# RWKV's 64-row products on all four quarters of the array, and retention scores of two heads in turn

## The chip, the cores and the metric

The kernel runs on one core of one Trainium2 chip. The metric is device microseconds of one execution. Before the change the median of three runs is 1125.02 us (1124.61 to 1125.1).

## What is computed

Two decoder layers on a sequence of 256 tokens with 1024 channels, in fp32. Each layer has a mixing part, a cross-attention into 256 memory tokens, and an MLP of 4096. The mixing part projects the normalised input once and hands the columns to four branches of 256 channels each (4 heads of 64): sparse attention, retention, RWKV-7, and a short convolution. Each branch is projected to 1024 channels, gated, summed, and projected once more.

The change touches two branches. RWKV-7, per head, token by token:

```python
def step(state, inp):
    r_t, w_t, k_t, v_t, kk_t, a_t = inp
    sa = jnp.einsum('bhvk,bhk->bhv', state, -kk_t)
    state = (state * w_t[:, :, None, :]
             + sa[..., None] * (kk_t * a_t)[:, :, None, :]
             + v_t[..., None] * k_t[:, :, None, :])
    return state, jnp.einsum('bhvk,bhk->bhv', state, r_t)
```

Retention, per head and chunk of 128 tokens:

```python
att = jnp.einsum('bhld,bhmd->bhlm', qc, kc) * inner_decay
o = (jnp.einsum('bhlm,bhmd->bhld', att, vc)
     + jnp.einsum('bhld,bhde->bhle', qc, state) * q_decay[None, :, :, None])
```

## The kernel before, in words

**The large matmuls.** Nearly all weights are streamed as units of 512 KB and split on the chip into a high part (ScalarE) and a low part (VectorE), both in the fp32r format; each product is three matmuls (`mm3`: high x high, high x low, low x high). They are the bulk of TensorE's work. In the profile they write tiles named `A`, `C` or `S`.

**The order.** Nothing runs in the order in which it is written. Every operation goes into a list (`Sched.add`) with a cost on its engine, and `Sched.run` plans the order: at each step it takes the operation that can start first by its model, and among those the one with the lowest rank. The projections have rank 9; RWKV is put in at rank 1 (its side products at 1.5), sparse attention at 2, retention at 3. So a product of RWKV goes as soon as its inputs are there, and the projections fill the time between. `together` makes one operation of several matmuls, which then follow each other on TensorE, and gives it one cost. The tiles `B` (two banks of PSUM at a time) are RWKV's, `C` those of sparse attention and retention.

**RWKV (`rwkv`).** The recurrence is done in chunks of 64 tokens: 256 tokens are two halves `t`, each of two chunks, and a tile of 128 partitions holds the even chunk on partitions 0 to 63 and the odd chunk on 64 to 127 (`par2`). The index `m = 4 t + h` (0 to 7) is the half and the head. All of it is plain fp32. Per layer and in the order of the work:

- scores `low` and `AL` (lines 1139 to 1149): for each head parity `s`, which is a half of the partitions of `ra` and `bb`, one group of 8 products of 64 x 64 x 64; each product writes to the chunk's half of the bank's partitions;
- `amat` (lines 1151 to 1163): the same with 128 columns, once for `AB` and, at rank 1.5 in `side`, once for `AK`, each as two groups of 8;
- the inverses of the 8-row blocks `R` and `RT` on VectorE and TensorE, which don't change;
- `mulc` (lines 1213 to 1221): 16 products of 64 x 64 x 64, the even chunk on rows 0 to 63 with its result on partitions 0 to 63 of one bank, the odd chunk on rows 64 to 127 with its result on partitions 64 to 127 of another bank. It makes the left half of the right side `rhs`, then `T1`, `RB` and `QB`;
- `RB` and `QB` are written as block-diagonal 128 x 128 matrices, zeros beside the blocks (four `memset` each, on GpSimd);
- `mul8` (lines 1205 to 1211): for each `m` one product of 128 x 128 x 128 with such a matrix, in two halves of four, each with its own bank and its own result. It makes `X1` and then, three times, `X = QB X + X1`; the sums are on VectorE;
- the states are carried from chunk to chunk (lines 1288 to 1317). After each odd chunk the output of both chunks of the half is made in one group: 16 products of 64 x 64 x 64, then the products of `ra` with the states, 128 rows by 64 by 128 columns (lines 1318 to 1332). The first chunk of all has no state.

**Retention (`ret`, lines 1536 to 1576).** For each head one bank of `C` takes the scores: a product of 64 x 128 x 256 and one of 64 x 128 x 128. Heads 0 and 2 lie on partitions 0 to 63, heads 1 and 3 on 64 to 127. The four heads are separate operations, so the planner orders them.

`self.act` is ScalarE's copy (line 621 in the profile), `self.tt` VectorE's two-operand operation (line 632), `self.vcopy` VectorE's copy (line 655), `self.mm` a matmul (line 675), `self.tr` a transpose on TensorE (line 680).

Of the kernel before, what the change touches and what calls it, by code (L numbers as in the profile page):

```python
# [14 lines left out]
OP = mybir.AluOpType  # L15
# [5 lines left out]
T = 256  # L21
# [234 lines left out]
class V:  # L256
# [32 lines left out]
    def step(self, name, d, *a, **k):  # L289
        return V(self.t, self.steps + ((name, a, k),), d, self.box, self.dtype).bound()  # L290
# [306 lines left out]
class Prog:  # L597
# [89 lines left out]
            self.group.append((cost, out, ins, emit, cols))  # L687

    @contextmanager
    def together(self):  # L690
        if self.group is not None:
            yield
            return
        self.group = g = []
        yield
        self.group = None
        if g:
            cost = i = 0
            while i < len(g):
                a, b = g[i][1], g[min(i + 1, len(g) - 1)][1]  # L700
                if a.shape[0] == b.shape[0] == 64 and a.box[0] != b.box[0]:
# [349 lines left out]
    def rwkv(self, l, zr, zk, zv, zl):  # L1051
# [85 lines left out]
        par2 = (slice(0, 64), slice(64, 128))  # L1137

        low, up = self.tile([128, 8, 64], "g2"), self.tile([128, 8, 64], "g2")
        for s, po in enumerate(par2):  # L1140
            p = B((128, 4, 64))
            with self.together():
                for t in range(2):
                    for a in range(2):
                        for pr in par2:
                            self.mm(p[pr, 2 * t + a], ra[po, a, t, 1, pr],
                                    bb[po, a, t * 128 + pr.start:t * 128 + pr.stop])
            self.tt(low[:, s::2], p, bcn("own8l", 4), OP.mult)
            self.tt(AL[:, s::2], p, bcn("low16", 4), OP.mult)

        def amat(dst, src, mask, first):
            for s, po in enumerate(par2):
                p = B((128, 4, 128))
                with self.together():
                    for t in range(2):
                        for a in range(2):
                            for pr in par2:
                                self.mm(p[pr, 2 * t + a].rearrange("p (i u) -> p i u", i=2),
                                        src[po, a, t * 128 + pr.start:t * 128 + pr.stop], ra[po, a, t, :, pr])
# [42 lines left out]
        for a in range(2):  # L1202
            self.ts(indr[:, 2 * a:2 * a + 2], c["head2"], pcol(l, "rk", 1, a), pool=True)

        def mul8(lhsT, rhs, evac):
            for q in range(2):
                p = B((128, 4, 128))
                for i in range(4):
                    m = 4 * q + i
                    self.mm(p[:, i], lhsT[:, m], rhs[:, m])  # L1210
                evac(slice(4 * q, 4 * q + 4), p)

        def mulc(lhsT, rhs, evac):

            ps = [B((128, 8, 64)) for _ in range(2)]
            with self.together():
                for m in range(8):
                    for pr, p in zip(par2, ps):
                        self.mm(p[pr, m], lhsT[pr, m], rhs(pr, m))
            for pr, p in zip(par2, ps):  # L1220
                evac(pr, p[pr])


        vt = g2()
# [10 lines left out]
        def side():  # L1235

            tokmajor(lambda a, t: ra[:, a, t, 1, :],
                     lambda p: [self.act(rhs[:, 4 * t:4 * t + 4, 64:128], p[:, t].rearrange("p (h k) -> p h k", h=4))
                                for t in range(2)])
            def stack(m, rows):  # L1240
                return lambda p: [self.act(m[rows, i::2], p[pr]) for i, pr in enumerate(par2)]

            tokmajor(lambda a, t: bb[:, a, t * 128:t * 128 + 128], stack(KB, par2[1]))
            tokmajor(lambda a, t: zv[:, a, t * 128:t * 128 + 128],
                     lambda p: (self.act(vt, p), stack(VU, par2[0])(p)))
            amat(AK, kt, "mask_k", False)
            tokmajor(lambda a, t: kt[:, a, t * 128:t * 128 + 128], stack(KB, par2[0]))
            mulc(AK[:, :, 1, :], lambda pr, m: vt[pr, m // 4, 64 * (m % 4):64 * (m % 4) + 64],
                 lambda pr, p: self.act(rhs[pr, :, 0:64], p))
            p = B((128, 2, 4))  # L1250
            for t in range(2):
                for a in range(2):
                    self.mm(p[:, t, 2 * a:2 * a + 2], rk[:, a, t * 128:t * 128 + 128], indr[:, 2 * a:2 * a + 2])
            bon = self.small(8)
            self.vcopy(bon, p.rearrange("p t h -> p (t h)"))
            self.bon = bon

        self.at(1.5, side)
        T1 = self.tile([128, 8, 64], "g2")
        mulc(AB[:, :, 1, :], lambda pr, m: R[pr, m],  # L1260
             lambda pr, p: self.vcopy(T1[pr], p) if pr.start else self.act(T1[pr], p))
        RB, QB = (self.tile([128, 8, 128], "g4") for _ in range(2))
        for m in (RB, QB):
            for i in range(2):
                self.s.lead(self.memset(m[64 * i:64 * i + 64, :, 64 - 64 * i:128 - 64 * i], 0.0))
        mulc(T1, lambda pr, m: RT[pr, m], lambda pr, p: self.tt(RB[pr, :, pr], p, RT[pr], OP.add))
        mulc(AL, lambda pr, m: RB[pr, m, pr],
             lambda pr, p: self.vcopy(QB[pr, :, pr], p) if pr.start else self.act(QB[pr, :, pr], p))
        X1 = self.tile([128, 8, 128], "g4")
        mul8(RB, rhs, lambda s, p: self.act(X1[:, s], p))  # L1270
        X = self.tile([128, 8, 128], "g4")
        for i in range(3):
            mul8(QB, X if i else X1, lambda s, p: self.tt(X[:, s], p, X1[:, s], OP.add))
        self.dump("X", X)
        MTt = g2()
        mcs = []
# [13 lines left out]
        for ci in range(4):  # L1290
# [25 lines left out]
                for a in range(2):  # L1316
                    self.stt(Sn[:, a], src[:, a], P1[:, a, ci, 64:65], c["bd"], OP.mult, OP.mult)
            if par == 1:
                ys = [(pr, St, B((128, T))[pr]) for pr, St in zip(par2, (Sprev, S))]
                with self.together():  # L1320
                    for h in range(4):
                        hs, m = slice(64 * h, 64 * h + 64), 4 * t + h
                        for pr, St, y in ys:
                            self.mm(y[:, hs], AK[pr, m, 0, :], vt[pr, t, hs], h == 0, False)
                        for pr, St, y in ys:
                            self.mm(y[:, hs], AB[pr, m, 0, :], U[pr, t, hs], False, St is None and h == 3)
                    for a in range(2):
                        for pr, St, y in ys:
                            if St is not None:
                                self.mm(y[:, a * 128:a * 128 + 128], ra[:, a, t, 0, pr], St[:, a], False, a == 1)  # L1330
                for pr, _, y in ys:
                    self.act(o[pr, t], y)
            Sprev = S
            if ci < 3:
                S = Sn
# [200 lines left out]
    def ret(self, l):  # L1536
# [17 lines left out]
        o = COFF["dec"][0]  # L1554
        self.dma(dec.rearrange("p h m -> p (h m)"), self.cst[:, o:o + H * T])
        o = self.tile([128, 2, T], "g2")
        for h in range(4):
            a, po = h // 2, slice(64 * (h % 2), 64 * (h % 2) + 64)
            hs = slice(64 * h, 64 * h + 64)
            p = self.bank("C")  # L1560
            self.mm(p[:, 0:256], k[po, a, 0:128], q[po, a])
            self.mm(p[:, 256:384], k[po, a, 128:256], q[po, a, 128:256])
            at = self.tile([128, 384], "g2")
            self.tt(at[:, 0:256], p[:, 0:256], dec[:, h], OP.mult)
            self.tt(at[:, 256:384], p[:, 256:384], dec[:, h, 0:128], OP.mult)
            y = self.bank("C", (128, 2, 64))
            self.mm(y[:, 0], at[:, 0:128], tk1[:, 0, hs], True, True)
            self.mm(y[:, 1], at[:, 128:256], tk1[:, 0, hs], True, False)
            self.mm(y[:, 1], at[:, 256:384], tk1[:, 1, hs], False, True)
            self.act(o[:, :, hs], y)  # L1570
# [547 lines left out]
```

## Time and profile before

| | before |
|---|---|
| median of three runs | 1125.02 us |
| the profiled execution | 1125.16 us |
| its span, first to last instruction | 1123.4 us |
| TensorE busy (matmul records) | 1107.5 us, 99% |
| VectorE busy | 857.0 us, 76% |
| ScalarE busy | 653.2 us, 58% |
| GpSimd busy | 98.8 us, 9% |
| granted TensorE clock, mean | 0.998 |

In a row of the profile `B<-g,g 64*64 64x128 f32 x32` reads: written tile `B`, read tiles `g` and `g`, weights of 64 rows by 64 columns, moving data of 64 partitions by 128 columns, 32 records. A matmul of fp32 leaves two records, one of fp32r a single one. In the timeline, records in a row that write and read tiles of the same names are merged into one line with the form of the first; a line gives the start and the time until the last of them has ended. Records overlap, so the distance from the start of a line to the start of the next is the time that it takes in the stream. Times are in us from the start of the span.

### The profile page before, as it was taken

What the parts mean: (1) busy time and instruction counts of PE and PEld (TensorE: products, weight loads), DVE (VectorE), ACT (ScalarE), POOL (GpSimd) and SP (SyncE); (2) the same over time, 40 slices, a digit from 0 to 9 for tenths busy, and PEclk for the clock granted to TensorE, in tenths of its full rate; (3) what the DMA queues carried; (4) which work ended last, traced back from release to release, by engine and by line L of the source; (5) the groups of instructions that cost most, each with busy time, mean ns of one, the idle gap of its engine ahead of it and who ended that gap; (6) DMA issues with size and microseconds to landing.
All of it is one profiled execution on the core that took longest, in us unless ns stands there. A gap on an engine that the chain in (4) does not pass through costs nothing.

```text
span 1123.4 us, 19170 instructions
## 1 busy us (share of the span) xinstructions
PE 1107.5 (99%) x7354; PEld 976.4 (87%) x7354; DVE 857.0 (76%) x1318; ACT 653.2 (58%) x1049; POOL 98.8 (9%) x163
## 2 busy tenths in 40 slices
PE   9999999999999999999999999999999999999996
PEld 7899978788998899999889999988888987999995
DVE  5878785675858689888796689755757667998987
ACT  7555544545645567767664566444547455776673
POOL 3001010100200110000021001000002002000000
PEclk9999999999999999999999999999999999999999
DMA  8327546754537599998955154565655467899981
GB/s 328 118 72 242 172 152 191 257 189 150 187 131 244 185 278 270 264 275 244 295 168 156 35 182 155 183 189 187 226 185 170 144 217 216 249 267 281 260 255 51
DMA packets 75967, 225.26 MB, mean 201 GB/s; under 512 B 12223, under 2 KB 14015, under 8 KB 75748
## 3 DMA queue, kind: packets, MB, share of 16 engines
q1 hardware_dynamic: 71556, 208.31, 55.1%
q0 software_dynamic: 4320, 15.73, 8.5%
q8 instruction: 58, 0.95, 0.3%
q14 instruction: 33, 0.27, 0.1%
HBM read 221.90 MB, written 3.15 MB: 200 GB/s over the span
## 4 chain that ended last, share of the span: by engine, by line
PE 72%; DVE 3%; DMA 2%; ACT 2%; POOL 1%; issue 1%; POOLq 0%; DVEq 0%; SPq 0%; ACTq 0%
PE A L675 34%; PE C L675 17%; PE S L675 12%; PE B L675 8%; DMA g<-wts 2%; PE C L680 2%; DVE g L632 1%; ACT junk L621 1%; ACT g L621 1%; POOL s L644 1%; DVE x L638 0%; POOL s L666 0%; ACT hi L621 0%; DVE lo L632 0%; PE B L680 0%
## 5 line engine op out<-in xcount | busy, mean ns | idle before, releaser
L632 DVE TENSOR_TENSOR lo<-raw,hi 128x1024 fp32r<-128x1024 f32 (+1 forms) x308 | 368.7, 1213 | 99.3 <-ACT hi L621 73.4
L621 ACT ACTIVATE hi<-raw 128x1024 fp32r<-128x1024 f32 (+1 forms) x308 | 316.4, 1049 | 121.0 <-PE A L675 70.4
L675 PE MATMUL A<-hi,g 128*128 128x512 f32 (+2 forms) x1152 | 366.9, 389 | 0.8 <-ACT g L621 0.5
L675 PEld LDWEIGHTS A<-hi,g 128*128 128x128 f32 x1152 | 215.2, 188 | 46.9 <-issue 1.5
L675 PE MATMUL A<-lo,g 128*128 128x512 f32 (+2 forms) x576 | 221.2, 384 | 0.0
L632 DVE TENSOR_TENSOR g<-g,g 128x512 f32<-128x512 f32 (+3 forms) x218 | 188.2, 887 | 10.1 <-ACT g L621 8.8
L675 PE MATMUL A<-g,hi 128*128 128x256 f32 x928 | 177.6, 291 | 0.0
L621 ACT ACTIVATE g<-g 128x1024 fp32r<-128x1024 f32 (+7 forms) x224 | 147.6, 698 | 49.5 <-DVE g L632 23.8
L675 PE MATMUL C<-g,hi 128*128 128x256 f32 x960 | 173.1, 282 | 0.5 <-ACT g L621 0.5
L675 PEld LDWEIGHTS C<-g,hi 128*128 128x128 f32 x960 | 149.7, 188 | 3.2 <-ACT g L621 0.9
L675 PEld LDWEIGHTS A<-g,hi 128*128 128x128 f32 x928 | 143.9, 189 | 6.1 <-issue 4.3
L675 PE MATMUL C<-g,lo 128*128 128x256 f32 x480 | 135.7, 283 | 0.0
L621 ACT ACTIVATE g<-C 128x512 fp32r<-128x512 f32 (+4 forms) x119 | 59.4, 515 | 127.3 <-PE C L675 100.8
L675 PE MATMUL A<-g,lo 128*128 128x256 f32 x464 | 130.7, 282 | 0.4 <-DVE lo L632 0.4
L675 PEld LDWEIGHTS A<-lo,g 128*128 128x128 f32 x576 | 108.5, 188 | 20.7 <-issue 0.5
L675 PE MATMUL S<-g,g 128*128 128x512 f32 x450 | 109.8, 394 | 0.1
L675 PEld LDWEIGHTS S<-g,g 128*128 128x128 f32 x450 | 84.4, 188 | 20.3 <-DVE g L632 0.5
L675 PEld LDWEIGHTS C<-g,lo 128*128 128x128 f32 x480 | 90.4, 188 | 0.0
L675 PEld LDWEIGHTS A<-g,lo 128*128 128x128 f32 x464 | 87.7, 189 | 0.6 <-DVE lo L632 0.6
L621 ACT ACTIVATE g<-A 128x512 f32<-128x512 f32 (+3 forms) x70 | 39.8, 569 | 60.7 <-PE A L675 59.3
L675 PE MATMUL B<-g,g 64*64 64x64 f32 (+4 forms) x896 | 67.6, 253 | 0.8 <-DVE g L632 0.8
L675 PEld LDWEIGHTS B<-g,g 64*64 64x64 f32 (+2 forms) x896 | 58.8, 151 | 6.4 <-issue 1.4
(143 smaller groups left out, 1076.1 us busy)
## 6 DMA issues: line engine op xcount, KB each, us to landing
raw<-wts SPq DMA_DIRECT2D x300, 512.0 KB, 4.5
g<-wts SPq DMA_DIRECT2D x90, 256.0 KB, 5.4
g<-wts POOLq DMA_DIRECT2D x30, 512.0 KB, 5.8
g<-rows SPq DMA_DIRECT2D x11, 512.0 KB, 4.4
g<-memT SPq DMA_DIRECT2D x12, 256.0 KB, 6.0
g<-cmpw SPq DMA_DIRECT2D x4, 512.0 KB, 4.8
raw<-wts SPq DMA_DIRECT2D x4, 498.0 KB, 4.0
raw<-wts SPq DMA_DIRECT2D x4, 480.0 KB, 4.8
```

The costliest lines, as they stand in the source:

```text
L621: e = lambda: self.nc.scalar.activation(real(out), real(in_), func, bias=real(bias), scale=real(scale), accum_out=real(accum))
L632: f = lambda: e.tensor_tensor(real(out), real(a), real(b), op)
L644: f = lambda: e.tensor_scalar(real(out), real(a), real(s1), real(s2), op0=op0, **kw)
L675: e = lambda: self.nc.tensor.matmul(real(out), real(lhsT), real(rhs), start=start, stop=stop, skip_group_check=True)
L680: self.pe(0.109, out, [in_, self.ident], lambda: self.nc.tensor.transpose(real(out), real(in_), real(self.ident)), 128)
```

## The change

- `tiles` takes the place of the two loops over the head parity: the groups of both parities become one group, and within it the head parities (rows of the array) and the chunks (columns) change in turn, so that four products in a row lie on four different quarters of the array. Each parity keeps its own bank. `amat` uses it too.
- `quad` takes the place of `mulc` and `mul8`. Each of the 16 products (8 values of `m`, two chunks) is 64 x 64 x n. Even heads stay where they are: rows and result on the same half of the partitions, bank `pe`. Odd heads go to the other half: rows 0 to 63 to partitions 64 to 127 and the reverse, bank `po`. So an odd head's result lies on the other half of the partitions than its chunk.
- What follows copes with that: some results are kept on both halves (`T1s`, `QBs`, `X1s`, `Xs`, `RTs`), `mixed` takes the one that is needed, and `turn` copies a result back with two ScalarE copies of 64 partitions each. `RB` and `QB` are 64 x 64 blocks now, without zeros.
- The output group writes the even heads to one bank and the odd heads, turned, to another; the products with the states are cut into two of 64 columns.
- `together(True)` gives such groups a cost of a quarter of their columns.
- In `ret` the scores of two heads (partitions 0 to 63 and 64 to 127) become one group, in turn.

```diff
     @contextmanager
-    def together(self):
+    def together(self, quads=False):
...
+                if quads:
+                    cost += 4 * self.free(a) / 2400 + 0.01
+                    i += 3
-        for s, po in enumerate(par2):
-            p = B((128, 4, 64))
-            with self.together():
+        def tiles(src, n, dst):
+            with self.together(True):
                 for t in range(2):
                     for a in range(2):
-                        for pr in par2:
-                            self.mm(p[pr, 2 * t + a], ra[po, a, t, 1, pr],
-                                    bb[po, a, t * 128 + pr.start:t * 128 + pr.stop])
+                        for s, po in enumerate(par2):
+                            for pr in par2:
+                                self.mm(dst[s][pr, 2 * t + a], *src(t, a, po, pr))
...
-        def mul8(lhsT, rhs, evac):
-            for q in range(2):
-                p = B((128, 4, 128))
+        def quad(lhsT, rhs, n, swap=False):
+            pe, po = (B((128, 4, n)) for _ in range(2))
+            with self.together(True):
                 for i in range(4):
-                    m = 4 * q + i
-                    self.mm(p[:, i], lhsT[:, m], rhs[:, m])
-                evac(slice(4 * q, 4 * q + 4), p)
-        def mulc(lhsT, rhs, evac):
-            ps = [B((128, 8, 64)) for _ in range(2)]
-            with self.together():
-                for m in range(8):
-                    for pr, p in zip(par2, ps):
-                        self.mm(p[pr, m], lhsT[pr, m], rhs(pr, m))
-            for pr, p in zip(par2, ps):
-                evac(pr, p[pr])
+                    for pr in par2:
+                        self.mm(pe[pr, i], lhsT(pr, 2 * i), rhs(pr, 2 * i))
+                    for src, dst in zip(par2, par2[::-1]):
+                        self.mm(po[dst, i], lhsT(src, 2 * i + 1), rhs(src, 2 * i + 1))
+            return pe, po
+        at = lambda m: lambda pr, i: m[pr, i]
+        mixed = lambda m, odd: lambda pr, i: odd[pr, i // 2] if i % 2 else m[pr, i]
+        def turn(dst, src):
+            for d, s in zip(par2, par2[::-1]):
+                self.act(dst[d], src[s])
...
-            mulc(AK[:, :, 1, :], lambda pr, m: vt[pr, m // 4, 64 * (m % 4):64 * (m % 4) + 64],
-                 lambda pr, p: self.act(rhs[pr, :, 0:64], p))
+            pe, po = quad(at(AK[:, :, 1, :]), lambda pr, m: vt[pr, m // 4, 64 * (m % 4):64 * (m % 4) + 64], 64)
+            self.act(rhs[:, 0::2, 0:64], pe)
+            turn(rhs[:, 1::2, 0:64], po)
...
+        turn(RTs, RT[:, 1::2])
+        pe, po = quad(at(AB[:, :, 1, :]), at(R), 64)
+        self.vcopy(T1[:, 0::2], pe)
+        self.act(T1s, po)
+        ps = quad(mixed(T1, T1s), mixed(RT, RTs), 64, True)
+        for i, p in enumerate(ps):
+            self.tt(RB[:, i::2], p, RT[:, i::2], OP.add)
+        pe, po = quad(at(AL), at(RB), 64)
+        self.act(QBs, po)
+        self.vcopy(QB[:, 0::2], pe)
+        turn(QB[:, 1::2], po)
+        pe, po = quad(at(RB), at(rhs), 128)
+        self.act(X1s, po)
+        self.act(X1[:, 0::2], pe)
+        turn(X1[:, 1::2], po)
+        def step(lhsT, rhs, swap):
+            pe, po = quad(lhsT, rhs, 128, swap)
+            self.tt(X[:, 0::2], pe, X1[:, 0::2], OP.add)
+            self.tt(*((X[:, 1::2], po, X1[:, 1::2]) if swap else (Xs, po, X1s)), OP.add)
+        step(mixed(QB, QBs), mixed(X1, X1s), True)
+        step(at(QB), at(X), False)
+        step(mixed(QB, QBs), mixed(X, Xs), True)
...
+                ys = [B((128, 2, 64)) for _ in range(2)]
+                ends = {pr: par2[1 - i] for i, pr in enumerate(par2)}
+                with self.together(True):
+                    for i in range(2):
+                        for f, m, b in ((0, AK, vt), (1, AB, U)):
+                            for s, y in enumerate(ys):
+                                h = 2 * i + s
+                                hs = slice(64 * h, 64 * h + 64)
+                                for pr, St in zip(par2, (Sprev, S)):
+                                    self.mm(y[ends[pr] if s else pr, i], m[pr, 4 * t + h, 0, :], b[pr, t, hs],
+                                            f == 0 and i == 0, f == 1 and St is None and i == 1)
+                    for i in range(2):
+                        for pr, St in zip(par2, (Sprev, S)):
+                            for s, y in enumerate(ys):
+                                if St is not None:
+                                    self.mm(y[ends[pr] if s else pr, i], ra[:, i, t, 0, pr], St[:, i, 64 * s:64 * s + 64],
+                                            False, i == 1)
+                o4 = o[:, t].rearrange("p (i s k) -> p s i k", i=2, s=2)
+                self.act(o4[:, 0], ys[0])
+                turn(o4[:, 1], ys[1])
...
-            p = self.bank("C")
-            self.mm(p[:, 0:256], k[po, a, 0:128], q[po, a])
-            self.mm(p[:, 256:384], k[po, a, 128:256], q[po, a, 128:256])
+            if h % 2 == 0:
+                scores = {h + i: self.bank("C") for i in range(2)}
+                with self.together():
+                    for cs, ks, qs in ((slice(0, 256), slice(0, 128), slice(0, 256)),
+                                       (slice(256, 384), slice(128, 256), slice(128, 256))):
+                        for i in range(2):
+                            po = slice(64 * i, 64 * i + 64)
+                            self.mm(scores[h + i][:, cs], k[po, a, ks], q[po, a, qs])
+            p = scores[h]
```

## Rows read from the trace of the kernel before

**Rows 1.** Page, part 1: busy time of each engine

```profile
PE 1107.5 (99%) x7354; PEld 976.4 (87%) x7354; DVE 857.0 (76%) x1318; ACT 653.2 (58%) x1049; POOL 98.8 (9%) x163
```

**Rows 2.** Waits of TensorE: total us, times, longest us

```profile
PE C L675 <- DVE g L644: 1.4, 1, 1.4
```

**Rows 3.** Timeline of TensorE, layer 0: start us, length us, instructions

```profile
35.21 0.28 PE L675 MATMUL A<-g,lo 128*128 128x256 f32 x1
35.42 0.98 PE L675 MATMUL B<-g,g 64*64 64x64 f32 x32
36.33 1.02 PE L675 MATMUL C<-g,s 33*4 33x512 f32 x2
...
38.18 1.59 PE L675 MATMUL B<-g,g 64*64 64x128 f32 x32
39.70 0.50 PE L675 MATMUL A<-g,hi 128*128 128x256 f32 x2
...
52.74 1.09 PE L675 MATMUL B<-g,g 64*64 64x128 f32 x16
53.76 0.66 PE L680 MATMUL B<-ident,g 128*128 128x128 f32 x4
...
55.77 1.15 PE L675 MATMUL B<-g,g 64*64 64x64 f32 x32
56.84 0.50 PE L675 MATMUL A<-g,hi 128*128 128x256 f32 x2
57.18 0.28 PE L675 MATMUL A<-g,lo 128*128 128x256 f32 x1
57.30 0.40 PE L675 MATMUL A<-g,hi 128*128 128x256 f32 x2
```

**Rows 4.** Timeline of TensorE, layer 1, a `mul8` product

```profile
642.57 1.95 PE L675 MATMUL B<-g,g 128*128 128x128 f32 x16
644.28 0.39 PE L675 MATMUL A<-hi,g 128*128 128x320 f32 x1
644.51 0.31 PE L675 MATMUL A<-lo,g 128*128 128x320 f32 x1
644.66 0.31 PE L675 MATMUL A<-hi,g 128*128 128x320 f32 x1
```

**Rows 5.** Timeline of TensorE, layer 1, 32-column weights of the sparse attention

```profile
661.46 1.08 PE L675 MATMUL C<-g,lk 128*32 128x128 f32 x32
662.47 0.71 PE L675 MATMUL B<-g,g 128*128 128x128 f32 x4
```

**Rows 6.** Timeline of TensorE, layer 1, second output island

```profile
668.51 1.74 PE L675 MATMUL B<-g,g 64*64 64x64 f32 x40
670.18 0.66 PE L675 MATMUL C<-g,ck 128*128 128x64 f32 x4
```

**Rows 7.** Timeline of TensorE, layer 0, retention scores of two heads

```profile
147.62 0.93 PE L675 MATMUL C<-g,g 64*128 64x256 f32 x8
148.48 0.50 PE L675 MATMUL A<-hi,g 128*128 128x512 f32 x1
```

**Rows 8.** Timeline of TensorE, layer 1, retention scores of one head

```profile
703.58 0.92 PE L675 MATMUL C<-g,g 64*128 64x256 f32 x4
704.43 0.51 PE L675 MATMUL A<-g,hi 128*128 128x256 f32 x2
```

**Rows 9.** ScalarE groups by form: x count, then busy us, mean ns

```profile
L621 ACT ACTIVATE g<-B 64x512 f32<-64x512 f32 x20 | 11.8, 592 | 6.7 <-PE B L675 3.3 <-PE B L680 3.2
...
L621 ACT ACTIVATE g<-B 64x256 f32<-64x256 f32 x8 | 3.0, 377 | 2.8 <-PE B L675 2.8
```

**Rows 10.** Busy us of each engine in a stretch; columns PE, PEld, DVE, ACT, POOL

```profile
640.00:700.00 60.00, 60.00 (x561) 55.19 (x560) 53.47 (x118) 38.17 (x89) 4.89 (x10) 1.00 0.49 160
```

**Rows 11.** Timeline of TensorE, layer 1, transposes of RWKV's output and of the merge

```profile
683.73 0.60 PE L680 MATMUL B<-ident,g 128*128 128x128 f32 x4
...
819.43 0.60 PE L680 MATMUL C<-ident,g 128*128 128x128 f32 x4
```

More of the change, by code (lines that the diff above doesn't have):

```diff
@@ L700, in together @@
                 a, b = g[i][1], g[min(i + 1, len(g) - 1)][1]
-                if a.shape[0] == b.shape[0] == 64 and a.box[0] != b.box[0]:
+                if quads:
+                    cost += 4 * self.free(a) / 2400 + 0.01
+                    i += 3
+                elif a.shape[0] == b.shape[0] == 64 and a.box[0] != b.box[0]:
                     cost += (4 * self.free(a) + 128) / 2400
@@ L1139, in rwkv @@
         low, up = self.tile([128, 8, 64], "g2"), self.tile([128, 8, 64], "g2")
-        for s, po in enumerate(par2):
-            p = B((128, 4, 64))
-            with self.together():
+        def tiles(src, n, dst):
+            with self.together(True):
                 for t in range(2):
                     for a in range(2):
-                        for pr in par2:
-                            self.mm(p[pr, 2 * t + a], ra[po, a, t, 1, pr],
-                                    bb[po, a, t * 128 + pr.start:t * 128 + pr.stop])
+                        for s, po in enumerate(par2):
+                            for pr in par2:
+                                self.mm(dst[s][pr, 2 * t + a], *src(t, a, po, pr))
+        ps = [B((128, 4, 64)) for _ in par2]
+        tiles(lambda t, a, po, pr: (ra[po, a, t, 1, pr], bb[po, a, t * 128 + pr.start:t * 128 + pr.stop]), 64, ps)
+        for s, p in enumerate(ps):
             self.tt(low[:, s::2], p, bcn("own8l", 4), OP.mult)
@@ L1151, in amat @@
         def amat(dst, src, mask, first):
-            for s, po in enumerate(par2):
-                p = B((128, 4, 128))
-                with self.together():
[L1155 to L1159, printed above, removed]
+            ps = [B((128, 4, 128)) for _ in par2]
+            tiles(lambda t, a, po, pr: (src[po, a, t * 128 + pr.start:t * 128 + pr.stop], ra[po, a, t, :, pr]), 128,
+                  [p.rearrange("p m (i u) -> p m i u", i=2) for p in ps])
+            for s, p in enumerate(ps):
                 if first:
@@ L1203, in rwkv @@
             self.ts(indr[:, 2 * a:2 * a + 2], c["head2"], pcol(l, "rk", 1, a), pool=True)
-        def mul8(lhsT, rhs, evac):
-            for q in range(2):
-                p = B((128, 4, 128))
+        def quad(lhsT, rhs, n, swap=False):
+            pe, po = (B((128, 4, n)) for _ in range(2))
+            with self.together(True):
                 for i in range(4):
-                    m = 4 * q + i
-                    self.mm(p[:, i], lhsT[:, m], rhs[:, m])
-                evac(slice(4 * q, 4 * q + 4), p)
-        def mulc(lhsT, rhs, evac):
-            ps = [B((128, 8, 64)) for _ in range(2)]
-            with self.together():
-                for m in range(8):
-                    for pr, p in zip(par2, ps):
-                        self.mm(p[pr, m], lhsT[pr, m], rhs(pr, m))
-            for pr, p in zip(par2, ps):
-                evac(pr, p[pr])
+                    for pr in par2:
[8 more added lines that the diff above has]
+                self.act(dst[d], src[s])
         vt = g2()
@@ L1258, in rwkv @@
         self.at(1.5, side)
[L1259 to L1273, printed above, removed]
+        odd = lambda n, tag: self.tile([128, 4, n], tag)
+        T1, T1s, RTs = self.tile([128, 8, 64], "g2"), odd(64, "g1"), odd(64, "g1")
+        turn(RTs, RT[:, 1::2])
+        pe, po = quad(at(AB[:, :, 1, :]), at(R), 64)
+        self.vcopy(T1[:, 0::2], pe)
+        self.act(T1s, po)
+        RB, QB, QBs = self.tile([128, 8, 64], "g2"), self.tile([128, 8, 64], "g2"), odd(64, "g1")
+        ps = quad(mixed(T1, T1s), mixed(RT, RTs), 64, True)
[5 more added lines that the diff above has]
+        turn(QB[:, 1::2], po)
+        X1, X1s = self.tile([128, 8, 128], "g4"), odd(128, "g2")
+        pe, po = quad(at(RB), at(rhs), 128)
+        self.act(X1s, po)
+        self.act(X1[:, 0::2], pe)
+        turn(X1[:, 1::2], po)
+        X, Xs = self.tile([128, 8, 128], "g4"), odd(128, "g2")
+        def step(lhsT, rhs, swap):
[5 more added lines that the diff above has]
+        step(mixed(QB, QBs), mixed(X, Xs), True)
         self.dump("X", X)
@@ L1318, in rwkv @@
             if par == 1:
[L1319 to L1332, printed above, removed]
+                ys = [B((128, 2, 64)) for _ in range(2)]
[18 more added lines that the diff above has]
+                turn(o4[:, 1], ys[1])
             Sprev = S
@@ L1556, in ret @@
         o = self.tile([128, 2, T], "g2")
+        scores = {}
         for h in range(4):
-            a, po = h // 2, slice(64 * (h % 2), 64 * (h % 2) + 64)
+            a = h // 2
             hs = slice(64 * h, 64 * h + 64)
-            p = self.bank("C")
-            self.mm(p[:, 0:256], k[po, a, 0:128], q[po, a])
-            self.mm(p[:, 256:384], k[po, a, 128:256], q[po, a, 128:256])
+            if h % 2 == 0:
[7 more added lines that the diff above has]
+            p = scores[h]
             at = self.tile([128, 384], "g2")
```

## Prediction

> **What bounds the kernel now.** I read the page's busy shares first, for the engine that can be the limit: TensorE is busy 99% of a span of 1123.4 us, VectorE 76%, ScalarE 58% [rows 1]. A busy TensorE can still be one that waits, because matmul records overlap; so the waits come next. The longest entry of all is 1.4 us [rows 2]. TensorE is therefore fed almost everywhere, and what counts is the pitch: the time from the first record of a stretch to the first record of the next. That is read in the timeline, and there the RWKV products stand out as islands in the stream of projection matmuls. Every matmul of fp32 is two records there. The island of the first scores, 16 products of 64x64x64 (32 records), takes 36.33 - 35.42 = 0.91 us; that of the second, 64x64x128, 1.52; one half of the third (16 records) 1.02; a triangular product by `mulc`, 32 records, 1.07 [rows 3]. A `mul8` product, 16 records on the whole array, takes 1.71 [rows 4].
>
> How many quarters of the array work at a time is in these numbers. A `mul8` record of 128 columns takes 1.71 / 16 = 0.107 us and fills the array. In the third scores' half the 16 records run on two tiles of one row half: 8 x 0.107 = 0.85, which leaves 0.17 for start and drain, so two tiles side by side. `mulc` is the same with 64 columns: 16 pairs in 1.07 - 0.17 = 0.90. Two of four quarters are idle in all of them. The first scores show more: their 32 records have `mulc`'s shape and count but take 0.16 us less, and the second scores' 1.52 is less than two halves of 1.02. These are two groups on different row halves, written one after the other, and the second starts before the first has drained: there all four quarters ran for a while. An island of four column tiles (32 records of 128 columns, 128x32) takes 1.01 [rows 5], as long as 16 records on two tiles: four tiles in turn do work side by side.
>
> **The change, part by part.** The unit is time on TensorE, as nothing else is late. An island with all four quarters has 8 turns instead of 16. For 64 columns: 0.90 / 2 + 0.17 = 0.62 us; for 128 columns: 1.02, the measured half of the third scores with two more tiles beside it. Around a 64x64 island the stream loses time too: 0.21 instead of 0.12 us from the last projection record to it (35.21 to 35.42), 0.34 instead of 0.24 for the first two behind it (56.84 to 57.18), 0.19 in all [rows 3]. Behind a `mul8` island it is 0.23 instead of 0.15, so 0.08 [rows 4].
>
> Per layer, then:
> - First scores, 0.91 to 0.62: 0.29 saved. Second, 1.52 to 1.02: 0.50.
> - Third scores: two islands of 1.02 become one, and one border goes: 1.02 + 0.19 = 1.21.
> - Four `mulc` islands (the old right side, T1, RB, QB), 1.07 to 0.62: 4 x 0.45 = 1.80.
> - Four `mul8` islands (X1 and three steps), 1.71 + 0.08 to 1.02 + 0.19: 4 x 0.58 = 2.32. The zeros of the block-diagonal RB and QB are no longer multiplied.
> - Two output islands. Before, 16 products and the state products behind them take 1.67 [rows 6]. After, 0.62 for the 16; the state products are cut to 64 columns on two tiles, 8 records (0.22 + 0.17 = 0.39) for the first pair of chunks, where one state is still zero, 16 records (0.62) for the second. Saved 1.67 - 1.01 and 1.67 - 1.24: together 1.09.
> - Retention. One head's scores alone take 0.85; two heads that the planner happened to put side by side in layer 0 take 0.86 together [rows 7, 8]. Layer 1 has three islands of 0.85, one of which holds a part of the next head too, and that head's rest, which I put at two records and a start, 2 x 0.107 + 0.17 = 0.38: 2.93. Layer 0 has the pair, one of 0.85 and such a rest: 2.09. After, both take 2 x 0.86 = 1.72. Layer 1 saves 1.21 and two borders (0.38), 1.59; layer 0 saves 0.37 and one border, 0.56.
>
> Layer 0: 0.29 + 0.50 + 1.21 + 1.80 + 2.32 + 1.09 + 0.56 = 7.77. Layer 1: 7.21 + 1.59 = 8.80. Sum 16.6 us.
>
> **What is added.** The 64-partition copies of `turn`, and the second copies of T1, QB, X1 and RT on the other half. A ScalarE copy of 64x512 takes 0.59 us, of 64x256 0.38 [rows 9]; I count full 128 partitions the same. Per layer ScalarE had T1, QB and two for the right side (4 x 0.59), X1 (2 x 0.59), the output (4 x 0.38): 5.1. It gets RT's two (2 x 0.38, the nearest row), T1s and QBs (2 x 0.38), QB's turn (2 x 0.38), X1, X1s and X1's turn (4 x 0.59), the right side (3 x 0.38) and six small ones for the output (0.38 at most, each): at most 8.1, 3.0 more. VectorE loses some: two copies and two sums of 512 elements become 256. GpSimd loses eight memsets in the kernel. I cost all of this at nothing: ScalarE is busy 38 of 60 us even in the densest stretch [rows 10], and the chain it lengthens has room: the RWKV output is transposed at 683.7 in layer 1, while the merged branches, of which RWKV's is the last to be multiplied, leave only at 819.4 [rows 11]. A step now waits for both of its sums where `mul8` let a half go ahead; the planner fills that with projection records, as it does now. If that cover were gone, TensorE would wait there (third rival). No DMA moves; the weight queue asks for the same bytes, only earlier.
>
> The sum is made against the profiled execution: 1125.16 us, of which 1123.4 is the span and 1.8 lies around it. The median of the runs is 1125.02, so the two are the same within 0.02%. 1125.2 - 16.6 = **1108.6 us**.
>
> **A rule against the change.** In `quad` each result bank is written from both row halves at once, to different partitions. Before, every bank took the results of one row half only (`mulc` kept two banks for it), so no row shows two row halves in one bank; column tiles share a bank in [rows 3, 5], and row halves overlap in time with different banks in [rows 3, 7]. The price is bounded below by four quarters (1108.6) and above by one quarter at a time, the fourth rival. I take the low end, as the destinations never share a partition. The Trainium skill, "TensorEngine Tiling (Array Packing)", section "Gotcha 1: PSUM Pressure", says that different row tiles cannot access the same PSUM bank at the same time; by it the second or the fourth rival's time would come out.
>
> **The rivals.**
> - *Records start no closer than now.* No island of 64 columns averages less than 0.91 / 32 = 0.028 us per record over its length [rows 3]. If that is all that can be issued, the 64-column islands (seven a layer) stay at 0.91 instead of 0.62: 7 x 0.29 = 2.0 a layer given back, 1112.7. For it: no row is under it over a whole island. Against: the 0.16 us by which the first scores beat `mulc` means that three turns there held four records each instead of two, about 0.014 us a record. The Trainium skill, "TensorE: Matmul & The Clock Gate", section "Wait — 56ns, not 53.3ns?", has a rule of this kind: starts never come closer than about 25 ns, however small the matmul. By it such an island would take 32 x 0.025 + 0.17 = 0.97, as good as this rival; the first scores speak against it, for three turns.
> - *Two quarters at a time in `quad` and the outputs.* `mulc` then gains nothing; a `mul8` successor takes 1.71 + 0.17 + 0.19 = 2.07 against 1.79, 1.12 worse a layer; the outputs gain 0.19; scores and retention stay. Layer 0: 2.00 - 1.12 + 0.19 + 0.56 = 1.6; layer 1: 2.7. Total 4.3, 1120.9: the change hardly does what it says.
> - *The cover goes.* VectorE is busy 53.5 of 60 us from 640 to 700 [rows 10]. If splits of weights are late there, the savings behind T1 and RB turn into waits: QB 0.45, steps 2.32, outputs 1.09, 3.9 a layer; 7.7 in all, 1116.3. Against it: TensorE waits for nothing in this stretch now.
> - *Slower: quarters that share a bank take turns.* One at a time, `quad` at 64 columns takes 1.97 (0.90 more than now), at 128 columns 32 x 0.107 + 0.36 = 3.78 (1.99 more). Per layer 3.6 + 8.0, the outputs 1.6 worse, less 2.0 for the scores and 0.6 or 1.6 for retention: 10.6 + 9.6 = 20.2 us, 1145.4. The point from which it decides: between 16.6 saved with four at once and 20.2 lost with one, in proportion to the time of a turn, the sign changes at about 1.7 quarters on average.
>
> **How the numbers follow.** Forecast 0.60; closer starts not possible 0.12; cover gone 0.11; two at a time 0.07; one at a time 0.05; something else that eats the whole gain, as the planner orders everything anew, 0.05. The range 1104 to 1118 takes in the first three (0.83), and lets the sum err by a quarter on the good side, for borders that merge. A measurement of this kernel can tell about 0.2%, 2.3 us, from no change. Faster by more: 0.60 + 0.12 + 0.11 + 0.07, less a little for that last: 0.89. Same 0.05, slower 0.06.
>
> **What would show it.** Right: of the `B<-g,g` records those of 128x128x128 fall by 128 (four products of 16 records, two layers) and those of 64x64x128 rise by 256; a 64-column island of 32 records at 0.62 us to the next record, a 128-column one at 1.02; two heads of retention in 0.86 everywhere; waits of TensorE still near nothing. A 64-column island above 0.9 is the first rival, at 1.07 the second, near 2 the fourth. Islands as forecast, with new waits for ScalarE or VectorE beside them, would be the third. Wrong altogether: islands as forecast, no waits, and a span that stays.

## The result and the profile after

The changed kernel takes 1106.81 us (median of four runs, 1106.33 to 1109.39), against 1124.82 for the kernel before in four runs. The ratio is 0.9846, with a 95% interval of 0.9828 to 0.9863: 18.0 us faster, where 16.6 was forecast. The profiled execution took 1106.55, its span is 1104.6.

The page of the changed kernel, part 1, which answers to [rows 1]:

```profile
PE 1089.9 (99%) x7506; PEld 958.5 (87%) x7506; DVE 854.3 (77%) x1318; ACT 657.7 (60%) x1067; POOL 91.0 (8%) x155
```

TensorE is as full as before in a shorter span. ScalarE has 4.5 us more (653.2 before), less than the 6 that I allowed for two layers, and VectorE 2.7 less. The waits of TensorE, as in [rows 2], have not grown either: the rows of that view add up to 6.4 us, 7.3 before, and the longest is still 1.4 us. The longest three are:

```profile
PE C L675 <- DVE g L644: 1.4, 1, 1.4
PE C L846 <- DVE g L843: 1.2, 1, 1.2
PE C L680 <- DVE g L632: 1.2, 2, 1.0
```

So the time went where it was looked for, into the islands. The timeline of TensorE of the changed kernel, layer 0, with the islands that answer to [rows 3, 4, 6]: the first scores, the second scores, three triangular products, one of the four full products and the second output island.

```profile
34.99 0.69 PE L675 MATMUL B<-g,g 64*64 64x64 f32 x32
35.61 1.02 PE L675 MATMUL C<-g,s 33*4 33x512 f32 x2
...
38.92 1.10 PE L675 MATMUL B<-g,g 64*64 64x128 f32 x32
39.95 0.50 PE L675 MATMUL A<-g,hi 128*128 128x256 f32 x2
...
63.62 0.69 PE L675 MATMUL B<-g,g 64*64 64x64 f32 x32
64.25 0.41 PE L675 MATMUL A<-hi,g 128*128 128x320 f32 x1
...
65.78 0.69 PE L675 MATMUL B<-g,g 64*64 64x64 f32 x32
66.41 0.50 PE L675 MATMUL C<-g,g 128*128 128x256 f32 x2
...
68.15 0.69 PE L675 MATMUL B<-g,g 64*64 64x64 f32 x32
68.78 0.74 PE L675 MATMUL C<-g,g 128*128 128x512 f32 x2
...
70.32 1.10 PE L675 MATMUL B<-g,g 64*64 64x128 f32 x32
71.36 0.42 PE L675 MATMUL A<-hi,g 128*128 128x320 f32 x1
...
99.66 1.31 PE L675 MATMUL B<-g,g 64*64 64x64 f32 x48
100.90 0.44 PE L675 MATMUL C<-g,ck 128*128 128x64 f32 x2
```

Start to next start: 0.62 or 0.63 for 32 records of 64 columns, 1.03 or 1.04 for 128 columns, 1.24 for the output island. The forecast had 0.62, 1.02 and 1.24. One island is longer, the right side in layer 0:

```profile
60.22 0.33 PE L675 MATMUL B<-g,g 64*64 64x64 f32 x4
60.82 0.68 PE L675 MATMUL B<-g,g 64*64 64x64 f32 x28 [0.27 <-DVE g L632]
61.43 0.41 PE L675 MATMUL A<-hi,g 128*128 128x320 f32 x1
```

It starts with the even heads, whose masked scores are ready, and then waits for VectorE's mask of the odd ones: 1.21 us instead of 0.63, about 0.6 us lost, once. This comes from the plan and not from the grouping: in layer 1 the same island takes 0.63, and in the run with a quarter of the planned cost (below) it takes 0.63 in layer 0 too.

The distances to the next record, summed over all records of a shape in the two traces (my sums), give the account:

| records | before, us | after, us | difference |
|---|---|---|---|
| `B`, 128x128x128 | 22.31 | 8.54 | -13.77 |
| `B`, 64x64x128 | 7.13 | 12.41 | +5.28 |
| `B`, 64x64x64 | 14.75 | 9.33 | -5.42 |
| `B`, 128x64 (states) | 7.87 | 6.83 | -1.04 |
| `C`, 64x128 (retention scores) | 5.08 | 3.41 | -1.67 |
| these together | 57.14 | 40.52 | -16.62 |
| all, with everything else | | | -18.75 |

These rows hold every record of a shape, also those that the change left alone. The changed islands by themselves take 43.01 us before and 27.16 after, 15.9 less (sums over both traces, island by island). The rest of the 16.62 is nearly all in the products that carry the states: 0.7 us, over half of which other records that now stand among them take up again. A wait of 0.83 us that the kernel before had for VectorE, ahead of a full product of layer 0, is gone:

```profile
72.07 2.05 PE L675 MATMUL B<-g,g 128*128 128x128 f32 x16 [0.83 <-DVE g L632]
```

The record counts moved as forecast; the forms (count, then busy us, mean ns) have 24 records of 128x128x128, where there were 152, and 384 of 64x64x128, where there were 128. Before, then after:

```profile
L675 PE MATMUL B<-g,g 128*128 128x128 f32 x152 | 19.4, 276 | 0.8 <-DVE g L632 0.8
...
L675 PE MATMUL B<-g,g 64*64 64x128 f32 x128 | 7.5, 275 | 0.0
```

```profile
L675 PE MATMUL B<-g,g 64*64 64x128 f32 x384 | 13.2, 275 | 0.0
...
L675 PE MATMUL B<-g,g 128*128 128x128 f32 x24 | 3.6, 274 | 0.0
```

Nearly all of the gain is made in the mixing parts, and it is kept. The first scores of layer 1, which start at 609.95 before, start at 600.35 now, 9.6 us earlier; of the other 9.2 us, 8.9 have come when that layer's branches are merged (819.4 before). Only 0.4 us are there before the first changed record, in the kernel's first matmuls. Before, then after:

```profile
609.95 0.97 PE L675 MATMUL B<-g,g 64*64 64x64 f32 x32
```

```profile
600.35 0.69 PE L675 MATMUL B<-g,g 64*64 64x64 f32 x32
600.98 0.39 PE L675 MATMUL A<-g,hi 128*128 128x256 f32 x1
```

### The profile page after: what moved, and what is told of

Its sections match the earlier page's. It is cut to its first block, busy times and chain, and to the rows that moved or that the text cites. A ratio compares the mean times of both kernels' runs of the same rounds, so it can differ in the third digit from the quotient of the medians.

```text
span 1104.6 us, 19483 instructions
## 1 busy us (share of the span) xinstructions
PE 1089.9 (99%) x7506; PEld 958.5 (87%) x7506; DVE 854.3 (77%) x1318; ACT 657.7 (60%) x1067; POOL 91.0 (8%) x155
## 4 chain that ended last, share of the span: by engine, by line
PE 92%; DVE 2%; ACT 2%; DMA 1%; POOL 1%; issue 1%; SPq 0%; POOLq 0%; DVEq 0%; ACTq 0%
PE A L675 47%; PE C L675 20%; PE S L675 13%; PE B L675 9%; PE C L680 2%; DMA g<-wts 1%; ACT junk L621 1%; DVE g L632 1%; DVE lo L632 1%; DVE x L638 1%; DVE g L638 0%; ACT g L621 0%; DMA x<-x 0%; POOL s L644 0%; POOL s L666 0%
## 5 line engine op out<-in xcount | busy, mean ns | idle before, releaser
L621 ACT ACTIVATE g<-C 128x512 fp32r<-128x512 f32 (+5 forms) x119 | 59.4, 514 | 122.5 <-PE C L675 93.8
L728 POOL DMA_DIRECT2D g<-wts x30 | 26.4, 880 | 330.8 <-DMA g<-wts 174.1
L675 PE MATMUL S<-hi,g 128*128 128x512 f32 x152 | 53.1, 394 | 0.0
```

What stands on the lines that cost most here:

```text
L621: e = lambda: self.nc.scalar.activation(real(out), real(in_), func, bias=real(bias), scale=real(scale), accum_out=real(accum))
L675: e = lambda: self.nc.tensor.matmul(real(out), real(lhsT), real(rhs), start=start, stop=stop, skip_group_check=True)
L728: f = lambda: self.nc.gpsimd.dma_start(real(out), in_, accum_op=OP.add)
```

## The experiments

The theory: TensorE is the limit, and every microsecond by which an island is shorter is a microsecond of the kernel. The rivals: the gain comes from the new plan of everything; the additions on ScalarE cost something; TensorE would find free quarters in any order; records can't start closer than a certain distance. Each run is compared with the kernel before on its own chip, and the ratios are what to compare; the changed kernel's is 0.9846 [0.9828, 0.9863].

**The products in another order.** Inside `quad`, and nothing else:

```diff
                 for i in range(4):
                     for pr in par2:
                         self.mm(pe[pr, i], lhsT(pr, 2 * i), rhs(pr, 2 * i))
+                for i in range(4):
                     for src, dst in zip(par2, par2[::-1]):
```

> In the new product routine the eight even-head products come first and the eight odd-head ones after them, instead of four quarters in turn; all else as changed. Theory (a quarter is only used if its product stands close behind in the stream): islands as long as the first scores of the kernel before, 0.91 for 64 columns and 1.52 for 128, so 4 x 0.29 + 4 x 0.49 = 3.1 us a layer worse than the changed kernel, about 1113. Rival (TensorE finds the free quarters itself, in whatever order the products stand): islands stay at 0.63 and 1.03, and the time at 1107.

Measured: ratio 0.9911 [0.9897, 0.9926], 1115.46 us. The timeline of TensorE in layer 0 has two triangular products and a full one:

```profile
65.84 0.97 PE L675 MATMUL B<-g,g 64*64 64x64 f32 x32
66.75 0.51 PE L675 MATMUL C<-g,g 128*128 128x256 f32 x2
...
68.50 0.97 PE L675 MATMUL B<-g,g 64*64 64x64 f32 x32
69.40 0.73 PE L675 MATMUL C<-g,g 128*128 128x512 f32 x2
...
70.94 1.59 PE L675 MATMUL B<-g,g 64*64 64x128 f32 x32
72.46 0.41 PE L675 MATMUL A<-hi,g 128*128 128x320 f32 x1
```

The islands are 0.90 or 0.91 and 1.52 long, as expected; these are the very times of the first and second scores before. The products, banks, copies and plan are the same: all 7506 records of TensorE stand in the same order of tiles and shapes as in the changed kernel. Over 40% of the gain is gone (0.0065 of 0.0154). Of the 8.4 us by which the profiled span is longer, 5.9 lie in these islands: it is the order that fills the quarters. Most of the rest is one wait ahead of layer 1, for a transfer of weights:

```profile
594.91 0.46 PE L675 MATMUL B<-g,g 128*128 128x256 f32 x1 [1.68 <-DMA g<-lora]
```

Whether the order has anything to do with that wait was not tried, so a third of the gain is what the order is shown to be worth in these products.

**Pieces of 32 and of 16 columns.** Each 64-column product of `quad` is cut:

```diff
+                step = 32 if n == 64 else n
                 for i in range(4):
+                    for j in range(0, n, step):
+                        js = slice(j, j + step)
                         for pr in par2:
-                            self.mm(pe[pr, i], lhsT(pr, 2 * i), rhs(pr, 2 * i))
+                            self.mm(pe[pr, i, js], lhsT(pr, 2 * i), rhs(pr, 2 * i)[:, js])
...
```

> The eight 64-column islands of the new product routine have each product cut into two of 32 columns: 64 records instead of 32, each with its own load of the weights. Theory (a turn is never shorter than the load of 64 columns of weights, half of the 0.101 us that records of 2 columns with 128 columns of weights take): 16 turns of 0.05 to 0.058, an island of 1.0 to 1.1. If columns alone counted: 0.62. If records could start no closer than 0.025 us on average: 64 x 0.025 + 0.17 = 1.77. The whole kernel is 3 to 4 us over the changed one by the theory.

> The same with pieces of 16 columns, 128 records an island. Theory (the load of the weights is the turn): 32 turns of 0.05 to 0.058, 1.8 to 2.0. Columns alone: 0.62. Starts no closer than 0.025 us: 128 x 0.025 + 0.17 = 3.4.

Measured, one run each: 1110.8 and 1119.84 us. A triangular product in the timeline of the first and of the second:

```profile
66.83 1.14 PE L675 MATMUL B<-g,g 64*64 64x32 f32 x64
67.89 0.38 PE L675 MATMUL C<-g,g 128*128 128x256 f32 x1
```

```profile
64.88 2.06 PE L675 MATMUL B<-g,g 64*64 64x16 f32 x128
66.86 0.41 PE L675 MATMUL A<-hi,g 128*128 128x320 f32 x1
```

1.06 and 1.98 us. Less the 0.17 for start and drain that is 0.89 / 64 = 0.014 us a record, and 1.81 / 128 = 0.014 again, over a whole island: starts can come that close for as long as there is work. A turn of four records takes the same 0.056 us with 32 columns and with 16, and 0.45 / 8 = 0.056 with 64, so below 64 columns something else than the columns sets it. Both times fit the load of the weights, which is the same in all three; a test with other weights was not made.

**ScalarE's copies three times.**

```diff
         def turn(dst, src):
-            for d, s in zip(par2, par2[::-1]):
-                self.act(dst[d], src[s])
+            for _ in range(3):
+                for d, s in zip(par2, par2[::-1]):
+                    self.act(dst[d], src[s])
```

> Every turn of an odd head's result to the other half is done three times over. That adds 24 copies of 64 partitions a layer, about 10 us of ScalarE each layer. Theory (ScalarE and the RWKV chain have room): within 0.3% of the changed kernel, 1106 to 1110. Rival (the turns lie on the path, or ScalarE holds up the splits of weights): up to 20 us more, 1115 to 1127.

Measured: ratio 0.9853 [0.9839, 0.9868], 1108.69 us. The page, part 1:

```profile
PE 1091.7 (99%) x7506; PEld 958.0 (87%) x7506; DVE 855.4 (77%) x1318; ACT 675.5 (61%) x1115; POOL 100.9 (9%) x155
```

ScalarE is busy 17.8 us longer (48 more instructions), and the intervals of the two ratios overlap almost wholly. What the change adds on ScalarE, a quarter of that, costs nothing that can be measured.

**Scores and retention alone.** The kernel before with `tiles` and with the pairs of heads; `mulc`, `mul8` and the outputs as before (the diff is those parts of the diff above).

> The changed score groups and the pairs of retention heads, but the triangular and the full products and the outputs as before. Theory (TensorE is the limit and each island gives what its length gives): the scores save 0.29 + 0.50 + 1.21 a layer, retention 0.56 and 1.59, so 6.2 us less than before: about 1118.7, with the old islands of 1.07 and 1.71 still in the trace. Rival (the gain comes from the new order of everything, and not from the islands): a time that has nothing to do with this sum, near 1107 or near 1125.

Measured: ratio 0.9966 [0.9955, 0.9977], 1121.84 us: 3.8 us instead of 6.2. Its islands are as short as in the changed kernel; here the second scores, 1.04:

```profile
39.45 1.10 PE L675 MATMUL B<-g,g 64*64 64x128 f32 x32
40.49 0.51 PE L675 MATMUL A<-g,hi 128*128 128x256 f32 x2
```

By my sums over the trace the records concerned are 5.0 us shorter, but the span is only 2.5 us shorter. What is missing is in TensorE's waits: the rows of the view add up to 10.6 us here and to 7.3 in the kernel before, and 1.1 of the difference stands in the first matmuls of the kernel, ahead of any changed record. So the expectation failed by 2.4 us, and not in the islands. The rest of the change then gave 14.2 us in place of the 10.4 forecast for it. Parts of the sum can't be had singly to better than some 2 to 4 us: each edit changes the plan of the whole kernel. Which of the two plans is the odd one was not settled.

**Retention as before.**

```diff
-            if h % 2 == 0:
-                scores = {h + i: self.bank("C") for i in range(2)}
-                with self.together():
...
+            p = self.bank("C")
+            self.mm(p[:, 0:256], k[po, a, 0:128], q[po, a])
+            self.mm(p[:, 256:384], k[po, a, 128:256], q[po, a, 128:256])
```

> The changed kernel with retention's scores as before, one head at a time. Theory: the 0.56 and 1.59 us of the sum come back, 1109.0. Rival (the planner puts heads side by side by itself now, as it did for two in layer 0): no difference, 1106.8.

Measured: ratio 0.9848 [0.9832, 0.9865], 1108.37 us: nothing lost that can be told from the changed kernel, though the theory's 2.15 us would be 0.0019 in the ratio, hardly more than the interval leaves open. The timeline of TensorE shows why. Three of the four pairs of heads stand side by side here too, two in layer 0 and one in layer 1:

```profile
148.39 0.93 PE L675 MATMUL C<-g,g 64*128 64x256 f32 x8
149.25 0.50 PE L675 MATMUL A<-hi,g 128*128 128x512 f32 x1
...
152.81 0.93 PE L675 MATMUL C<-g,g 64*128 64x256 f32 x8
153.67 0.50 PE L675 MATMUL A<-hi,g 128*128 128x512 f32 x1
...
705.96 0.93 PE L675 MATMUL C<-g,g 64*128 64x256 f32 x8
706.82 0.50 PE L675 MATMUL A<-hi,g 128*128 128x512 f32 x1
```

In this plan both heads are ready when TensorE gets to them. By my sums the records of the scores take 4.06 us in this run, 5.08 in the kernel before and 3.41 in the changed one: of the 1.67 us, 1.0 comes with the rest of the change, and 0.65 with retention's own edit.

**What the planner is told.** Four runs change nothing but the planned cost of the new groups:

```diff
 # as measured: 0.34 us more for each group (a second run: 1.0 instead of 0.34)
-            cost = i = 0
+            cost, i = 0.34 * quads, 0
 # planned as two quarters
-                if quads:
+                if False:
 # a quarter of the cost
-                    cost += 4 * self.free(a) / 2400 + 0.01
+                    cost += self.free(a) / 2400
```

> The changed kernel, but the planner is told 0.34 us more for each new group: the start, the drain and the border that the trace of the changed kernel shows (0.625 us to the next record where the plan has 0.47). Nothing else differs. Theory (the plan only fills, and TensorE is fed either way): 1106 to 1108. Rival (the new cost, and the order that follows from it, is part of the gain or of what is left): more than 2.5 us away from 1106.8, faster if the one island that waited 0.58 us in layer 0 is a sign of a plan that comes too early.

> The changed kernel, but the planner still takes the new groups for products of two quarters, 0.16 us a pair. The products stand in their group as in the changed kernel. Theory (quarters are a matter of the array, not of the plan): islands of 0.63 and 1.03, 1106 to 1109. Rival (the cost in the plan makes the gain): back towards 1125.

> The changed kernel with 1.0 us added to the planned cost of each new group, so that the plan has an island of 64 columns at 1.47 and one of 128 at 1.89, where the trace shows 0.63 and 1.03 and 0.19 of border. This is the error of the run planned as two quarters, in one number and without its rule for pairs. Theory (a plan that takes TensorE for busy longer than it is puts products into the stream before their inputs are there, and TensorE, which can't change its order, waits): 1112 to 1118, islands as short as before but new waits in them and around them. Rival (something else in that run, as how it counts the cut state products, made it slow): 1106 to 1109.

> The changed kernel with the planned cost of the new groups at a quarter: 0.11 us for an island of 64 columns and 0.21 for one of 128. Theory (an error on this side makes TensorE late against the plan, the inputs are there early, and nobody waits): 1106 to 1109. Rival (any error of the plan costs): 1110 to 1116.

| planned cost | ratio | 95% | us |
|---|---|---|---|
| a quarter | 0.9834 | [0.9819, 0.9849] | 1106.78 |
| as changed | 0.9846 | [0.9828, 0.9863] | 1106.81 |
| 0.34 us more, as measured | 0.9848 | [0.9831, 0.9864] | 1108.03 |
| as two quarters | 0.9900 | [0.9885, 0.9915] | 1114.21 |
| 1.0 us more | 0.9907 | [0.9892, 0.9922] | 1114.94 |

The second expectation of these failed: I had taken the plan for a mere filler. Planned as two quarters, the kernel loses 6 to 7 us of its 18 with the same islands on the array. The run with 1.0 us more repeats that without the rule for pairs, and so excludes the cut state products as its cause. Its timeline in layer 0:

```profile
61.37 0.69 PE L675 MATMUL B<-g,g 64*64 64x64 f32 x32
62.80 0.38 PE L675 MATMUL C<-g,g 128*128 128x256 f32 x1 [0.74 <-ACT g L621]
63.92 0.39 PE L675 MATMUL C<-g,g 128*128 128x256 f32 x1 [0.73 <-DVE g L632]
...
65.47 1.13 PE L675 MATMUL B<-g,g 64*64 64x64 f32 x32
66.54 0.79 PE L675 MATMUL C<-g,g 128*128 128x256 f32 x2
...
69.00 0.69 PE L675 MATMUL B<-g,g 64*64 64x64 f32 x32
69.62 0.41 PE L675 MATMUL A<-hi,g 128*128 128x320 f32 x1
```

An island is over after 0.69 us where the plan has 1.47; the next product stands there as if its input had had another 0.8 us, and TensorE waits 0.74 for ScalarE and 0.73 for VectorE. The island at 65.47 is longer (1.07 instead of 0.63) for another reason. TensorE was busy for only 0.53 of the 2 us from 62 to 64, and then the granted clock is at its lower level (0.50, that is 1.2 GHz instead of 2.4) for 3.4 us; the projection records beside the island are as slow, 0.27 us from the one at 67.13 to the next where 0.15 is usual. The column behind POOL is the granted clock:

```profile
62.00:64.00 2.00, 0.53 (x7) 0.27 (x2) 1.13 (x4) 1.12 (x3) 0.00 (x0) 1.00 0.00 0
65.00:68.00 3.00, 3.00 (x40) 2.41 (x39) 2.93 (x9) 1.62 (x7) 0.00 (x0) 0.50 0.02 5
```

That is about 1.7 us of this run's loss. In the run planned as two quarters the clock stays at 1.00 until TensorE has finished, and the loss is there all the same: it is waits in the first place. The rows of the view add up to 10.4 us here and to 11.7 planned as two quarters, against 6.4 in the changed kernel; the spans are 7.7 and 8.1 longer. Some islands also wait between their records, and the rest of the difference was not traced singly.

In the other direction nothing is lost, though the error is no smaller. With its border of 0.19 an island takes 0.82 or 1.22 us; the plan has 1.47 and 1.89 in the run with 1.0 us more, and 0.11 and 0.21 in the run with a quarter.

**A third bank.** `NPS = {"A": 4, "B": 3, ...}` instead of `"B": 2`.

> The changed kernel with three banks of PSUM for the tiles of RWKV instead of two, so that a side product needn't wait until both banks of an island are read. Theory (TensorE is fed either way): 1106 to 1108. Rival (the two banks that an island takes at once delay the chain or the side products): 1104 or less.

Measured: ratio 0.9847 [0.9830, 0.9864], 1107.65 us. No difference that can be told: that an island takes both banks at once doesn't show in the time. No run beat the changed kernel by more than the intervals.

## Why the prediction was right

- **The bound.** Right. TensorE at 99% with hardly a wait meant that its stream is the time, and the pitch from start to next start was the right thing to read. The profile after has the same 99%.
- **Four quarters at a time.** Right, and it could be read beforehand: the 0.16 us between the first scores and `mulc`, and the 32-column islands. The run with two then two turns that reading round: it gives the islands of the first scores back exactly (0.91).
- **The sizes.** Islands alone were to save 16.5 us (the 16.6 of the sum with its borders left out, where they nearly cancel); the changed islands gave 15.9, and nearly all of the 0.6 between is the one island that waited. That the rows of the table come to 16.62 is luck: they hold other records of the same shapes. The eight full products were to give 8 x 0.69 = 5.5; they took 13.72 together before and 8.27 after, 5.45 less. The 64-column records gave 5.42 where 6.0 was forecast, for the same island. Retention gave 1.67 for 1.58, but more through the plan than through the edit.
- **The 1.4 us beyond.** The sum's error is the difference of 18.0 and 16.6; in the two profiles it is more, as the span fell by 18.75, 2.9 more than the islands. In these 2.9 are the 0.4 at the kernel's start and one wait of 0.83 that is gone, ahead of a full product of layer 0 in the kernel before; the forecast had neither. How the other 1.6 divide between borders that merge and small products was not settled, and four runs of the changed kernel differ by 3 us.
- **What was costed at nothing.** Right: three times the turns cost no time that can be told, and ScalarE grew by less than the bound.
- **The rivals.** Less start and drain, records start 0.014 us apart for a whole island (0.45 / 32), so the first rival is out; the rule of the Trainium skill, "TensorE: Matmul & The Clock Gate", section "Wait — 56ns, not 53.3ns?", of about 25 ns between starts does not hold here between different quarters. Two quarters at a time (1.07) and one (near 2) are out by the islands of 0.62, in which each of the banks `pe` and `po` is written from both row halves. The rule of the Trainium skill, "TensorEngine Tiling (Array Packing)", section "Gotcha 1: PSUM Pressure", that row tiles can't access one bank at the same time, does not bind where they write different partitions; the same partitions were not tried. The cover held, but for two new waits of 0.3 us for VectorE, one of them in the island shown above.
- **What the prediction left out.** It put a chance of 0.05 on the planner's new order and called the plan what fills the time. The plan's cost of a group is a part of the change that is worth a third of it: the sum holds only with a planned cost that isn't much too long, a condition that the prediction doesn't name. Told 1.0 us more for each group, the planner would have given 1114.9 us with the same islands.

## What to carry to other kernels

Where TensorE's records follow without waits, count how many of its quarters an island uses. Take the time from the island's start to the next start, less start and drain (0.17 us here), and divide it by the time of one turn, which is that of one record on its tile (0.107 us for 128 columns of fp32 here, 0.056 for 64). The number of records divided by the number of turns is the number of quarters that work at a time. Small products that stand in turn on different quarters run side by side; standing in two blocks they do so only in part (0.91 us instead of 0.62 for the 64-column islands), though nothing else differs. In a kernel whose order is planned from costs, change the cost together with the product: a plan that is too long is paid for in waits, one that is too short costs nothing here.

## What the runs showed that I had not expected

The asymmetry of the plan: about 7 us lost with 1.0 us more per group, nothing with three quarters of the cost missing. That waits can cost more than themselves: after two of 0.7 us the granted clock was 0.50 for 3.4 us. And that a turn of four records doesn't shrink below 0.056 us, with 64, 32 or 16 columns alike, so that the 64-column products are just at the size where cutting further gains nothing.
